# A hybrid decoder step on one core: steps of four chains issued at other ticks, and the last rows scaled by another engine

## The chip, the cores and the metric

The kernel runs on one core of a Trainium2 chip. A core has five engines with a queue of instructions each: TensorE (PE; its weight loads are shown apart as PEld), VectorE (DVE), ScalarE (ACT), GpSimd (POOL) and SyncE (SP), which here does nothing but issue DMAs. An engine takes its instructions in the order of the program and waits, with all that stands behind, when one of them has to wait for another engine or a DMA. The metric is the device time of one execution in microseconds (us), the median of several runs. Nothing is done on the host but to lay out the inputs.

## What is computed

One step of a two-layer decoder in float32 for a prompt of 512 tokens and for 8 samples of one token each (520 columns), width 1024. Cut to what the change comes near:

```python
# layer 0: h = rmsnorm(x) * (1 + scale) + shift;  z = h @ w_in
bg, cg, xv, ga, q, k, v, gb = split(z)
y_a = bg * conv3(cg * xv) * silu(ga)
# prompt: for (window, dilation) in (128,1), (512,4), (2048,16): causal softmax attention,
#         merged by the softmax denominators; samples: one query each against a cached window
y_b = dilated_attention(q, k, v) * silu(gb)
x = x + gate * (concat(y_a, y_b) @ w_out)
# layer 1: same wrapper
u, gc, q, k, v, gd = split(rmsnorm-modulated x @ w_in)
y_c = (pool_mix(u) * pool_scale) * silu(gc)
# retention, 4 heads of 256: prompt in chunks; samples:
new_state = exp(log_g) * state + outer(k, v)
y_d = per_head_norm(q @ state ...) * silu(gd)
x = x + gate * (concat(y_c, y_d) @ w_out)
y = rmsnorm(x, norm_f)
```

Outputs are the two `y`, the appended rows of the convolution, of the windows and of the pooling, and the retention states.

## The kernel before

**Products.** Activations are held transposed: 128 features on the partitions, 520 columns along them. Each weight tile of 1024 x 128 is loaded by SP (`wraw`, 512 KB), split by ACT into a high part (`whi`) and by DVE into a low part (`wlo`), so that float32 accuracy comes from three passes (high x high, high x low, low x high). A product of one weight tile is eight steps k of six matmuls, two column halves times three passes, into one of two PSUM tiles (`mm2`, tag `mm`). So a product needs the PSUM tile of the one before last to have been read. All else on PE uses four smaller PSUM buffers (`aux`).

**Order.** The order of the program is written out by the kernel itself: nothing reorders it. Behind each k step `tick()` counts one tick and issues what is due between the matmuls of the products: everything in `timed` (`at(dt, ...)`), one entry of `side` (`put(..., after=n)`), or, when none of `side` is due, one of `fill` (`put_fill`), and on even ticks one of `aside` (`put2`). So a step's tick is its place in each engine's queue, and all instructions that the step issues, for PE, DVE, ACT or SP, stand at that place.

**Stages, in order of time.**

1. Eight head pairs (`head_pair(p)`), four products each: values, keys, gate, queries. At the end of the query product the pair's attention is put into `side` by ticks counted from there, `Q0 = 5` plus n: two `score` steps (n = 0 and 4), three `turns` (11, 13, 16: PE transposes the softmaxed blocks, ACT makes their high part, DVE their low part a tick or two later), and eight `weigh(e, i)` (L699): values times weights for the pair's two heads e, in four parts i. `weigh(e, 2)` reads group 2, from the last `turns`, `weigh(e, 3)` ends with an ACT copy and a DVE add. They run inside the next pair's products. `q_lo` (L690) is the DVE step that makes the queries' low part and reads the query product's PSUM tile. `ada_two` (32 matmuls for layer 1's modulation) waits in `fill`; for the last pair it is put there 25 ticks after the query product.
2. Layer 0's convolution: 32 products, `a_tile(i, m)` with i from 0, each of which first calls what `hook(i, ...)` left for it. Among them is the softmax of the samples' window scores, in three steps: `soft_scores` (put at i = 5), `soft_turn` and `soft_new`, each put by the one before. `soft_scores` begins with a product of queries and keys on DVE (`prod`), which a matmul with `on_d` sums.
3. Layer 0's output projection (`out_tile`), which sums the squares of the new x (`sqa`).
4. The seam: layer 1's first products run on unnormalised input, while `r1_sums`, `r1_roots` and `rms_rows` make the row factors `r1`, a tick apart, which the evictions (`z_first`) then read. `r1_sums` is put by `at(3, ...)` (L960).
5. Retention, four heads (`ret_head(h)`): values 2 products, keys 2, queries 2, gates 2. The samples' states are loaded four at a time (`state_load`), and `state_new(b0, i)` makes the new state of one sample: ACT scales the old one, DVE makes two products with the v rows `vb`, which have gone through DRAM (`vdr`) to be spread over all partitions; the fourth issues the stores on SP three ticks later. The first four are put into `aside` at the end of the second key product (L1181), the other four after the queries.
6. Pooling, then the output projection of layer 1, whose rows are transposed and scaled by `norm_f` as they come. The last product is done in two column halves; after each, `rows_scale` (L1323) makes 1/rms of its row blocks and scales each block of 128 rows by it, in two half rows (`xo[i][0]`, `xo[i][1]`) that are then stored. The last call is for blocks 0 and 1.

Of the kernel before, what the change touches and what calls it, by code (L numbers as in the profile page):

```python
# [13 lines left out]
ACTF = mybir.ActivationFunctionType  # L14
ALU = mybir.AluOpType
# [3 lines left out]
P = 128  # L19
# [67 lines left out]
def hybrid_kernel(ctx: ExitStack, tc: tile.TileContext, a, o):  # L87
    nc = tc.nc
# [3 lines left out]
    def mk(pool, shape, dt, tag, bufs=None):  # L92
        n_made[0] += 1
        return pool.tile(shape, dt, name=f"{tag}_{n_made[0]}", tag=tag, bufs=bufs)
# [10 lines left out]
    def tt(n=T, dt=F32, p=P):  # L105
        n_made[0] += 1
        return tp.tile([p, 530], dt, name=f"t_{n_made[0]}", tag="t")[:, 0:n]
# [14 lines left out]
    def aux(shape):  # L122
        return mk(auxp, shape, F32, "aux")
# [10 lines left out]
    def act(out, in_, func=ACTF.Copy, bias=None, scale=1.0, accum_out=None):  # L134
        kw = {}
        if bias is not None:
            kw["bias"] = bias
        if accum_out is not None:
            kw["accum_out"] = accum_out
        return nc.scalar.activation(out=out, in_=in_, func=func, scale=scale, **kw)  # L140

    def vcopy(out, in_):
        return nc.vector.tensor_copy(out, in_)  # L143

    def vtt(out, in0, in1, op):
        return nc.vector.tensor_tensor(out=out, in0=in0, in1=in1, op=op)  # L146

    def stt(out, in0, scalar, in1, op0, op1):
        return nc.vector.scalar_tensor_tensor(out=out, in0=in0, scalar=scalar, in1=in1, op0=op0, op1=op1)  # L149

    def vts(out, in0, s1, s2, op0, op1=None):
        if op1 is None:
            return nc.vector.tensor_scalar(out=out, in0=in0, scalar1=s1, scalar2=None, op0=op0)
        return nc.vector.tensor_scalar(out=out, in0=in0, scalar1=s1, scalar2=s2, op0=op0, op1=op1)

    def load(out, in_):
        return nc.sync.dma_start(out=out, in_=in_)

    def mm(out, lhsT, rhs, start, stop):
        nc.tensor.matmul(out, lhsT=lhsT, rhs=rhs, start=start, stop=stop)  # L160
# [23 lines left out]
    def at(dt, fn, *args):  # L184
        seqn[0] += 1
        heapq.heappush(timed, (now[0] + dt, seqn[0], fn, args))

    def put(fn, *args, after=0):
        seqn[0] += 1
        heapq.heappush(side, (now[0] + after, seqn[0], fn, args))  # L190
# [4 lines left out]
    def put2(fn, *args):  # L195
        aside.append((fn, args))
# [316 lines left out]
    def head_pair(p):  # L513
# [182 lines left out]
            put(score, blocks, after=Q0 + n)  # L696
        for g, n in enumerate((11, 13, 16)):
            put(turns, g, after=Q0 + n)
        for e, ticks in ((0, (18, 19, 20, 21)), (1, (22, 23, 24, 26))):  # L699
            for i, n in enumerate(ticks):  # L700
                put(weigh, e, i, after=Q0 + n)

# [7 lines left out]
    for p in range(KT):  # L710
        if p == 6:
            load(scv, a["conv_t"])
        head_pair(p)
# [9 lines left out]

    soft = {}

    def soft_scores():

        prod = tt(P).rearrange("p (b k e) -> p b k e", b=NB, k=KT)
        nc.gpsimd.memset(prod, 0.0)
        for e in range(2):  # L730
            r = slice(64 * e, 64 * e + 64)
            vtt(prod[r, :, :, e].rearrange("p b k -> p k b"), zs[0][r, 32:40, :], zs[0][r, 40:48, :], ALU.mult)
        st = aux([P, 257])
        for t in range(2):
            nc.tensor.transpose(st[:, t * P:(t + 1) * P], scores[:, t].rearrange("p b h -> p (b h)"), ident)
        mm(st[:, 256:257], prod.rearrange("p b k e -> p (b k e)"), on_d[:, 0:1], True, True)
        bd = csm[:, C_BD:C_BD + 257]
        sc = tt(257)
        stt(sc[:, 0:256], st[:, 0:256], 0.125, bd[:, 0:256], ALU.mult, ALU.add)
        stt(sc[:, 256:257], st[:, 256:257], 128.0, bd[:, 256:257], ALU.mult, ALU.add)  # L740
        sm = mk(cp, [P, 2], F32, "sm", 1)
        nc.vector.tensor_reduce(out=sm[:, 0:1], in_=sc, op=ALU.max, axis=AX.X, negate=True)  # L742
        act(sc, sc, ACTF.Exp, bias=sm[:, 0:1], accum_out=sm[:, 1:2])
        nc.vector.reciprocal(sm[:, 1:2], sm[:, 1:2])
        vts(sc, sc, sm[:, 1:2], None, ALU.mult)
        soft["sc"] = sc
        put(soft_turn, after=4)

    def soft_turn():
        sc = soft["sc"]  # L750
        pt_ = aux([P, 2, P])
        for t in range(2):
            nc.tensor.transpose(pt_[:, t, :], sc[:, t * P:(t + 1) * P], ident)
        vcopy(pT[:, :, 0:P], pt_)
        pnr = mk(cp, [P, 64], F32, "pnr", 1)
        vts(pnr, csm[:, C_BCR:C_BCR + 64], sc[:, 256:257], None, ALU.mult)
        soft["pnr"] = pnr
        put(soft_new, after=2)

    def soft_new():  # L760
        pnb = aux([P, 64])
# [53 lines left out]
    def hook(i, fn, *args):  # L815
        hooks.setdefault(i, []).append((fn, args))

    hook(5, put, soft_scores)
    for b0 in range(0, NB, 2):
        i = 5 + 3 * b0 - (2 if b0 else 0)  # L820
# [136 lines left out]
        act(h1[j][0], x)  # L957
        at(2, lo_of, h1[j][1], x, h1[j][0])

    at(3, r1_sums)  # L960
    for j in range(KT):
        at(H1A - 2 + H1B * j, h1_scale, j)
        at(H1A + H1B * j, h1_x, j)
# [21 lines left out]
    def ret_head(h):  # L985
# [192 lines left out]
            for part in range(2):  # L1178
                put(state, i, part, after=5 + (DK if h == 0 else 0))
        for i in range(4):  # L1180
            put2(state_new, 0, i)  # L1181
        for i in range(2):
            if i == 0:
                state_load(4)
# [28 lines left out]
    for h in range(H_D):  # L1213
        ret_head(h)
# [81 lines left out]
    xo = [[tt(512) for _ in range(2)] for _ in range(4)]  # L1296
# [4 lines left out]
    rs = cp.tile([P, 5], F32, name="rs")  # L1301
# [21 lines left out]
    def rows_scale(blocks):  # L1323
        i0, i1 = blocks[0], blocks[-1] + 1
        nc.vector.tensor_reduce(out=rs[:, i0:i1], in_=ss[:, i0:i1], op=ALU.add, axis=AX.X)
        act(rs[:, i0:i1], rs[:, i0:i1], ACTF.Sqrt, bias=eps[:, 0:1])
        nc.vector.reciprocal(rs[:, i0:i1], rs[:, i0:i1])
        for i in blocks:
            if i < 4:
                act(xo[i][0], xo[i][0], ACTF.Copy, scale=rs[:, i:i + 1])  # L1330
                vts(xo[i][1], xo[i][1], rs[:, i:i + 1], None, ALU.mult)
                for hf in range(2):
                    q = nc.scalar if i == 1 else nc.sync
                    q.dma_start(out=o["y_prompt"][0, i * P:(i + 1) * P, hf * 512:(hf + 1) * 512], in_=xo[i][hf])
            else:
                for hf in range(2):
                    vts(xos[hf], xos[hf], rs[0:NB, i:i + 1], None, ALU.mult)
                    load(o["y_sample"].rearrange("b s d -> (b s) d")[:, hf * 512:(hf + 1) * 512], xos[hf])
# [18 lines left out]
    for hf in (1, 0):  # L1357
        ps = mm2()
        for half in (1, 0):
            if hf == 1:  # L1360
                ws.append((take_w(("o", 1, half, m)), yhl[0:KT] if half else yhl[KT:]))
            w, hs = ws[1 - half]
            for k in range(KT):
                mm3(ps, w, k, hs[k][0], hs[k][1], half == 1 and k == 0, half == 0 and k == KT - 1, (hf,))
                if hf == 1:
                    advance(k)
                tick()
        x, g, c = xT[m], mG[1], slice(256 * hf, 256 * hf + 256)
        stt(x[:, c], ps[:, hf, 0:H0], g[:, m, 8:9], x[:, c], ALU.mult, ALU.add)
        if hf == 1:  # L1370
            tmp = mk(cp, [P, NB], F32, "gtmp", 2)
            vtt(tmp, ps[:, 1, H0:H0 + NB], g[:, m, 0:NB], ALU.mult)
            vtt(x[:, S:T], tmp, x[:, S:T], ALU.add)
        blocks = range(2) if hf == 0 else range(2, 5)
        at(4, rows, m, blocks)
        at(6, rows_scale, blocks)
# [71 lines left out]
```

## Time and profile before

| | |
|---|---|
| median of 3 runs (lowest, highest) | 1060.53 us (1060.45, 1061.29) |
| the profiled execution's own time | 1060.99 us |
| its span, from the first to the last instruction | 1058.9 us |
| mean granted clock of TensorE | 0.997 |
| read from HBM, written to it | 149.40 MB, 18.65 MB |

By the first matmul of each product the stages lie in the span about so: head pairs 26 to 285 (the last pair's attention runs on to 319), convolution 285 to 499, output projection 499 to 596, retention 596 to 849, pooling 849 to 953, the last projection 953 to 1050, scaling and storing to the end.

A row of a timeline is the start, the length, the engine, line, operation, the tiles written and read, their size, how many instructions were merged, and in brackets the idle time of the engine before it and what ended it. A row of the waits is the engine and line that waited, what it waited for, the total, how often, and the longest. A row of the windows gives for a stretch the busy time and number of instructions of PE, PEld, DVE, ACT and POOL, then the granted clock, the share of the DMA engines and GB/s. Lines are those of helpers (L160 every matmul, L140 every activation, L146 two-input DVE operations, L149 fused ones, L153 scalings), so the tiles tell the places apart.

### The profile page before, as it was taken

How to read it: one execution, taken by the hardware profiler on the slowest of the kernel's cores; microseconds unless marked ns; L12 is line 12 of the kernel's file. 1: busy time of each engine (PE TensorE's matmuls, PEld its weight loads, DVE VectorE, ACT ScalarE, POOL GpSimd, SP SyncE). 2: the span in 40 equal slices, each digit the busy share in tenths (PEclk: the TensorE clock that was granted, in tenths of full speed). 3: DMA queues.
4: the chain of work that ended last, by engine and by line, in shares of the span. 5: the costliest groups of instructions: out<-in, count | busy, mean ns of one | idle time of the engine just before them, and what ended most of it. 6: DMA issues, size and time to landing. Idle time of an engine off the chain costs nothing.

```text
span 1058.9 us, 21054 instructions
## 1 busy us (share of the span) xinstructions
PE 1034.0 (98%) x8682; PEld 989.6 (93%) x8682; DVE 623.8 (59%) x1470; ACT 485.6 (46%) x884; POOL 4.3 (0%) x33
## 2 busy tenths in 40 slices
PE   5999999999999999999999999999999999999996
PEld 3899999999999999999999998999999999999996
DVE  5656777667775444456344586665657576674443
ACT  5666567765654222224232474445444453333333
POOL 0000000000000000000000000000000000000000
PEclk9999999999999999999999999999999999999998
DMA  9576664576626635613744255363726523225322
GB/s 352 213 248 200 180 171 158 172 212 189 192 88 197 191 109 185 199 61 141 238 147 138 100 168 197 109 203 113 263 81 212 164 78 129 81 80 172 101 71 81
DMA packets 82175, 168.95 MB, mean 160 GB/s; under 512 B 7208, under 2 KB 47240, under 8 KB 79000
## 3 DMA queue, kind: packets, MB, share of 16 engines
q1 hardware_dynamic: 81792, 167.09, 49.0%
q8 instruction: 68, 1.11, 0.4%
q10 hardware_dynamic: 288, 0.52, 0.1%
q14 instruction: 27, 0.22, 0.1%
HBM read 149.40 MB, written 18.65 MB: 159 GB/s over the span
## 4 chain that ended last, share of the span: by engine, by line
PE 64%; DVE 2%; ACT 1%; DMA 1%; issue 0%; DVEq 0%; ACTq 0%
PE mm L160 55%; PE aux L160 8%; DVE t L146 1%; DMA v<-vdr 1%; DVE wlo L146 0%; ACT t L140 0%; PE aux L1318 0%; DVE big L149 0%; DVE t L149 0%; ACT whi L140 0%; PE aux L999 0%; PE aux L992 0%; DMA vdr<-t 0%; ACT v L140 0%; PE aux L374 0%
## 5 line engine op out<-in xcount | busy, mean ns | idle before, releaser
L160 PE MATMUL mm<-t,whi 128*128 128x256 f32 (+1 forms) x4608 | 755.0, 285 | 1.1 <-DVE zs L143 0.9
L160 PEld LDWEIGHTS mm<-t,whi 128*128 128x128 f32 x4608 | 636.2, 188 | 17.6 <-issue 13.6
L160 PE MATMUL mm<-t,wlo 128*128 128x256 f32 (+2 forms) x2304 | 465.4, 282 | 0.0
L160 PEld LDWEIGHTS mm<-t,wlo 128*128 128x128 f32 x2304 | 358.1, 188 | 0.0
L146 DVE TENSOR_TENSOR wlo<-wraw,whi 128x512 fp32r<-128x512 f32 x288 | 189.0, 683 | 57.7 <-ACT whi L140 57.0
L140 ACT ACTIVATE whi<-wraw 128x1024 fp32r<-128x1024 f32 x144 | 151.7, 1053 | 96.4 <-PE mm L160 53.9
L146 DVE TENSOR_TENSOR t<-t,t 128x520 fp32r<-128x520 f32 (+6 forms) x182 | 119.0, 657 | 98.7 <-ACT t L140 97.0
L140 ACT ACTIVATE t<-t 128x520 fp32r<-128x520 f32 (+3 forms) x116 | 71.0, 616 | 161.3 <-DVE t L149 102.9
L140 ACT ACTIVATE t<-aux 128x384 fp32r<-128x384 f32 (+7 forms) x156 | 67.8, 465 | 135.3 <-PE aux L160 79.1
L140 ACT ACTIVATE t<-mm 128x512 f32<-128x512 f32 (+2 forms) x116 | 56.2, 506 | 116.2 <-PE mm L160 114.8
L146 DVE TENSOR_TENSOR t<-aux,t 128x384 fp32r<-128x384 f32 (+6 forms) x120 | 58.4, 494 | 33.2 <-ACT t L140 28.3
L160 PE MATMUL aux<-t,v 128*128 128x512 f32 (+2 forms) x224 | 51.2, 327 | 1.1 <-DVE t L146 0.6
L160 PE MATMUL aux<-t,t 64*128 64x256 f32 (+6 forms) x384 | 51.9, 320 | 0.0
L143 DVE COPY zs<-mm 128x8 f32<-128x8 f32 x76 | 12.0, 158 | 64.5 <-ACT t L140 64.5
L160 PEld LDWEIGHTS aux<-t,t 64*128 64x128 f32 (+1 forms) x384 | 41.5, 186 | 3.9 <-issue 1.7
L140 ACT ACT_TABLE_LOAD x32 | 41.1, 1283 | 4.5 <-DVE sm L742 2.2
L160 PEld LDWEIGHTS aux<-t,v 128*128 128x128 f32 x224 | 35.1, 188 | 3.8 <-DVE t L146 2.7
L140 ACT ACTIVATE t<-t,mn 128x128 f32<-128x128 f32 (+3 forms) x64 | 35.1, 551 | 0.1
L149 DVE SCALAR_TENSOR_TENSOR big<-v,ksc,big 128x256 f32<-128x256 f32 x64 | 27.7, 480 | 12.0 <-ACT big L140 9.8
L146 DVE TENSOR_TENSOR t<-mm,t 128x512 f32<-128x512 f32 (+1 forms) x24 | 16.5, 689 | 30.4 <-PE mm L160 22.8
L591 DVE CUSTOM_DVE_ANT_0 t<-aux,t 128x128 f32<-128x128 f32 (+3 forms) x64 | 27.5, 486 | 10.7 <-PE aux L160 10.7
L146 DVE TENSOR_TENSOR gtmp<-mm,mG 128x8 f32<-128x8 f32 x16 | 2.6, 165 | 44.4 <-PE mm L160 44.4
(153 smaller groups left out, 552.4 us busy)
## 6 DMA issues: line engine op xcount, KB each, us to landing
wraw<-in_w_in_e SPq DMA_DIRECT2D x64, 512.0 KB, 3.9
wraw<-in_w_in_o SPq DMA_DIRECT2D x48, 512.0 KB, 3.4
big<-in_ada_e SPq DMA_DIRECT2D x12, 1024.0 KB, 8.6
big<-in_ada_o SPq DMA_DIRECT2D x12, 1024.0 KB, 10.3
wraw<-in_w_out_e SPq DMA_DIRECT2D x16, 512.0 KB, 3.3
big<-in_state_ret SPq DMA_DIRECT2D x16, 512.0 KB, 7.2
out_new_ret_sample<-big SPq DMA_DIRECT2D x16, 512.0 KB, 3.0
wraw<-in_w_out_o SPq DMA_DIRECT2D x16, 512.0 KB, 4.3
```

What stands on the lines that cost most here:

```text
L140: return nc.scalar.activation(out=out, in_=in_, func=func, scale=scale, **kw)
L143: return nc.vector.tensor_copy(out, in_)
L146: return nc.vector.tensor_tensor(out=out, in0=in0, in1=in1, op=op)
L149: return nc.vector.scalar_tensor_tensor(out=out, in0=in0, scalar=scalar, in1=in1, op0=op0, op1=op1)
L160: nc.tensor.matmul(out, lhsT=lhsT, rhs=rhs, start=start, stop=stop)
L591: nc.vector.tensor_tensor_reduce(out=sb, in0=s[:, 0:n], in1=bt[e][:, S - n:S], scale=1.0, scalar=3e38, op0=ALU.add, op1=ALU.min, accum_out=mn,
```

## The change

Four things are moved in the program's order, and the last scaling is divided otherwise.

- `weigh`: the parts of the first head are issued 18, 19, 21 and 22 ticks after `Q0` in place of 18, 19, 20 and 21, those of the second 23, 24, 25 and 27 in place of 22, 23, 24 and 26.
- The softmax: `prod` becomes a step of its own, `soft_prod`, which the fifth convolution product (i = 4) calls; `soft_turn` comes eight ticks after `soft_scores` (four before) and `soft_new` four after that (two before).
- `r1_sums` comes at the fourth tick in place of the third.
- `state_new` for the first four samples: with h = 0 it is put into `aside` eight ticks later, for other heads one tick later.
- `rows_scale`: ACT scales only the first half row of the odd blocks (1 and 3) and issues its store; DVE scales all other half rows, and SP issues their stores. Before, ACT scaled the first half row of each block and DVE the second, and SP issued all stores but those of block 1, which ACT issued.

```diff
-        for e, ticks in ((0, (18, 19, 20, 21)), (1, (22, 23, 24, 26))):
+        for e, ticks in ((0, (18, 19, 21, 22)), (1, (23, 24, 25, 27))):
             for i, n in enumerate(ticks):
                 put(weigh, e, i, after=Q0 + n)
...
-    def soft_scores():
+    def soft_prod():
 
         prod = tt(P).rearrange("p (b k e) -> p b k e", b=NB, k=KT)
         nc.gpsimd.memset(prod, 0.0)
         for e in range(2):
             r = slice(64 * e, 64 * e + 64)
             vtt(prod[r, :, :, e].rearrange("p b k -> p k b"), zs[0][r, 32:40, :], zs[0][r, 40:48, :], ALU.mult)
+        soft["prod"] = prod
+
+    def soft_scores():
+
+        prod = soft["prod"]
         st = aux([P, 257])
...
-        put(soft_turn, after=4)
+        put(soft_turn, after=8)
...
-        put(soft_new, after=2)
+        put(soft_new, after=4)
...
+    hook(4, soft_prod)
     hook(5, put, soft_scores)
...
-    at(3, r1_sums)
+    at(4, r1_sums)
...
         for i in range(4):
-            put2(state_new, 0, i)
+            at(1 if h else 8, put2, state_new, 0, i)
...
             if i < 4:
-                act(xo[i][0], xo[i][0], ACTF.Copy, scale=rs[:, i:i + 1])
-                vts(xo[i][1], xo[i][1], rs[:, i:i + 1], None, ALU.mult)
                 for hf in range(2):
-                    q = nc.scalar if i == 1 else nc.sync
-                    q.dma_start(out=o["y_prompt"][0, i * P:(i + 1) * P, hf * 512:(hf + 1) * 512], in_=xo[i][hf])
+                    dst = o["y_prompt"][0, i * P:(i + 1) * P, hf * 512:(hf + 1) * 512]
+                    if i % 2 and hf == 0:
+                        act(xo[i][hf], xo[i][hf], ACTF.Copy, scale=rs[:, i:i + 1])
+                        nc.scalar.dma_start(out=dst, in_=xo[i][hf])
+                    else:
+                        vts(xo[i][hf], xo[i][hf], rs[:, i:i + 1], None, ALU.mult)
+                        load(dst, xo[i][hf])
```

## The prediction

> **What bounds the kernel.** First the page: the share of each engine and the granted clock. Then who kept TensorE (PE) waiting, all over the span.
>
> ```profile
> span 1058.9 us, 21054 instructions
> PE 1034.0 (98%) x8682; PEld 989.6 (93%) x8682; DVE 623.8 (59%) x1470; ACT 485.6 (46%) x884; POOL 4.3 (0%) x33
> PEclk9999999999999999999999999999999999999998
> ```
>
> ```profile
> PE aux L160 <- DMA t<-in_x_t: 8.3, 1, 8.3
> PE aux L160 <- DVE t L146: 1.6, 4, 0.6
> PE mm L160 <- DVE zs L143: 0.9, 2, 0.7
> PE aux L753 <- DVE t L153: 0.6, 1, 0.6
> PE aux L1318 <- DVE t L149: 0.6, 1, 0.6
> PE aux L160 <- DVE pnr L153: 0.3, 1, 0.3
> ```
>
> PE is busy for 98% of the span at full granted clock, so no edit of DVE or ACT work counts by its own length: it counts where PE waits for it, or behind PE's last matmul. The columns of the waits are the total, how often, and the longest. The first row lies in the kernel's start, which the change doesn't touch. What is left is some 4 us in nine short waits, and the change touches most of the places. So the question is what those waits really cost, and whether moving the steps makes new ones.
>
> **How long a short wait is.** Here are three rows of PE's timeline in the last head pair (start, length, operation, and the idle time before it).
>
> ```profile
> 308.67 0.28 PE L160 MATMUL aux<-t,v 128*128 128x256 f32 x1
> 309.53 0.39 PE L160 MATMUL aux<-t,v 128*128 128x256 f32 x1 [0.59 <-DVE t L146]
> 310.48 0.40 PE L160 MATMUL aux<-t,v 128*128 128x256 f32 x2
> ```
>
> Two of these matmuls take 0.40, one takes 0.28, so undisturbed ones start 0.12 apart and each overlaps the next by 0.16. Across the wait the starts lie 0.86 apart, 0.74 more than 0.12, while the row prints 0.59. A wait therefore costs its printed idle time plus 0.16, and one under 0.16 prints nothing. I price every wait below so. The Trainium skill, Perfetto Trace Analysis, section "Identifying the Most-Contended Engine", says that matmul busy time misleads because matmuls are pipelined, and takes the weight loads' busy share instead; the 0.59 against 0.74 here agrees, and by its measure the next term would be 2.7 in place of 2.35 and the whole sum 6.9.
>
> **Weighted values, L699 (eight head pairs).** In each pair `weigh(0, 2)` needs the low part of the third group's transposes, which DVE makes late.
>
> ```profile
> PEld aux L160 <- DVE t L146: 2.7, 8, 0.8
> 314.75 1.93 PE L160 MATMUL aux<-big,scT 128*32 128x256 f32 x32
> big<-in_ada_o SPq DMA_DIRECT2D x12, 1024.0 KB, 10.3
> ```
>
> The first row is of the waits of PE's weight loads between 52 and 318 us: eight, one for each pair, 2.7 in all. The longest, 0.8, is the one above, 0.74 by its starts; I take 0.05 off each, so the other seven are 1.9 - 0.35 = 1.55, and with the last 0.75 I get 2.3. One tick is one k step of a product, six matmuls, 0.72. `weigh(0, 2)` issued a tick later finds the low part done in seven pairs (their mean wait is 0.22) and just about in the last. No instruction is added. What slides is the end: `weigh(1, 3)` now comes in the last tick of the query product, so its ACT copy stands before the query's eviction on ACT, and its DVE add before `q_lo`; I cost this at nothing, and its price is the fourth rival. In the last pair `ada_two` waits in `fill` for a free tick: before, that was tick 30 (the x32 row at 314.75), now it is 25, the tick freed in front of `weigh(0, 2)`. Its 1.93 of PE work and one ACT copy only change places; its weights are asked for 28 ticks, 20 us, ahead, and such a load takes 10.3 by the page's row above, so they are there. It gives `weigh(0, 2)` 1.9 more slack.
>
> **The convolution's softmax, L726 to L758.** PE stalls three times in one chain; the last row is DVE's.
>
> ```profile
> 326.17 0.35 PE L160 MATMUL aux<-on_d,t 128*128 128x1 f32 x2 [0.47 <-DVE t L146]
> 330.12 0.44 PE L753 MATMUL aux<-csm,t 128*128 128x128 f32 x2 [0.61 <-DVE t L153]
> 332.30 0.44 PE L160 MATMUL aux<-pnr,csm 128*128 128x64 f32 x2 [0.31 <-DVE pnr L153]
> 325.50 0.52 DVE L146 TENSOR_TENSOR t<-zs 64x64 f32<-64x64 f32 x2
> ```
>
> 0.47 + 0.61 + 0.31 and three times 0.16 make 1.87. `soft_prod` takes the two products (0.52) out of the chain and issues them eight ticks, 5.8, before the matmul that reads them; its fill on POOL goes past one or two short fills of that queue, which works 4.3 in the whole span by the page, so it delays none of them. `soft_turn` comes four ticks later, 2.9 against a wait of 0.77, and `soft_new` two more, 1.4 against 0.47. The next reader, the windows' weighing, is due at tick 65 and the chain now ends at 53. The 0.52 stays on DVE, beside PE's products. None of the three issues a DMA. I take all of 1.87 as gone.
>
> **Row sums of the seam, L960.**
>
> ```profile
> 599.08 1.28 PE L160 MATMUL aux<-on_d,t 128*128 128x1 f32 x10 [0.32 <-DVE t L146]
> 603.59 0.70 DVE L146 TENSOR_TENSOR t<-t,t 128x520 f32<-128x520 f32 x1 [0.34 <-ACT t L140]
> 605.40 0.69 DVE L149 SCALAR_TENSOR_TENSOR t<-mm,t 128x512 f32<-128x512 f32 x1 [1.11 <-PE mm L160]
> ```
>
> The wait is 0.48; one tick of 0.72 covers it. What is late next is `r1`, by 0.72 - 0.48 = 0.24: its first reader at 603.59 moves by that, and the first eviction that reads it (605.40) waits for PE by 1.11 anyway. Gain 0.48.
>
> **The first head's state, L1181.** PE rows, then DVE rows, the last one a group of the page (busy, mean ns of one).
>
> ```profile
> 638.74 0.72 PE L160 MATMUL mm<-t,whi 128*128 128x256 f32 x4 [0.74 <-DVE zs L143]
> 639.91 0.51 PE L160 MATMUL aux<-v,t 128*128 128x256 f32 x2 [0.21 <-ACT t L140]
> 640.63 0.74 PE L160 MATMUL aux<-v,t 128*128 128x256 f32 x4 [0.22 <-DVE t L146]
> 643.35 1.56 PE L160 MATMUL aux<-t,t 128*128 128x512 f32 x6
> 633.45 0.88 DVE L149 SCALAR_TENSOR_TENSOR big<-v,ksc,big 128x256 f32<-128x256 f32 x2 [1.32 <-DMA v<-vdr]
> 637.84 0.68 DVE L146 TENSOR_TENSOR t<-mm,t 128x512 fp32r<-128x512 f32 x1
> 638.44 0.15 DVE L143 COPY zs<-mm 128x8 f32<-128x8 f32 x1
> 641.70 0.68 DVE L146 TENSOR_TENSOR t<-mm,t 128x512 fp32r<-128x512 f32 x1
> L146 DVE TENSOR_TENSOR wlo<-wraw,whi 128x512 fp32r<-128x512 f32 x288 | 189.0, 683 | 57.7 <-ACT whi L140 57.0
> ```
>
> DVE stands 1.32 for the v rows that come back through DRAM, then makes four pairs of products before the first query's low part (637.84) and its sample copy (638.44); PE waits for that copy to get its PSUM tile back, then twice for k's split behind it: 0.74 + 0.21 + 0.22 and 0.48 make 1.65. Between 633.45 and 637.84 lie 4.39: the four pairs, some 0.8 each, and two weight splits (683 ns alone, some 0.6 in a row). With h = 0 put off by eight ticks, one pair stands before that copy and three behind it, and the splits fill the 1.32 of waiting: the copy ends at 638.59 - 2.4 - 1.2 = 635.0, ahead of PE's need near 637.9. What is late next: the second query's low part (641.70, done at 642.4), now behind the other three pairs; the work ahead of it is the same but 1.2 of idling is gone, so it ends near 641.2, and the first score, then at 643.35 - 1.65 = 641.7, needs it some 0.7 into its 1.56. Slack about 1. The two stores on SP follow their last step, six ticks later, past one weight load, which is asked for four tiles ahead. Other heads: steps leave the list on even ticks only, so one tick's delay leaves them where they were. Gain 1.65.
>
> **The tail, L1328.** ACT and DVE scale rows, SP and ACT issue the last four stores; below them the windows' row of the DMAs (the last number is GB/s).
>
> ```profile
> 1052.97 1.33 ACT L140 ACTIVATE t<-t,rs 128x512 f32<-128x512 f32 x2 [0.23 <-DVE rs L1327]
> 1052.97 0.88 DVE L153 TENSOR_SCALAR t<-t,rs 128x512 f32<-128x512 f32 x2
> 1053.72 0.83 SPq L1334 DMA_DIRECT2D out_y_prompt<-t  x2
> 1054.34 0.87 ACTq L1334 DMA_DIRECT2D out_y_prompt<-t  x2
> 1055.00:1056.00 1.00, 0.00 (x0) 0.00 (x0) 0.00 (x0) 0.00 (x0) 0.00 (x0) 0.50 1.03 383
> ```
>
> A half row takes ACT about 0.72 and DVE 0.48 (0.40 to the next). Before, the first store waits for ACT, 1053.72; now for DVE, 1053.48: 0.24 earlier. The last issue goes from 1054.80 (ACT's second) to 1054.40 (SP's third): 0.40 earlier. The DMA engines are full while the four stores run, 1 MB at 383 GB/s is 2.7, longer than the issues; so the start counts, 0.24, and 0.40 is the other end. DVE's extra half row among the earlier blocks (five in place of four, 0.40) ends near 1050.1, before the residual at 1050.34 that waits for PE. The Trainium skill, DMA: Bandwidth & Descriptors, section "Issuing engines are not separate DMA queues", says that DMAs of several issuers share the same engines and that a second issuer saves only issue time; this speaks against giving SP three of four. The trace agrees: with 383 GB/s moving, the issues (0.83 for two) run ahead of the data.
>
> **The sum.** 2.3 + 1.87 + 0.48 + 1.65 + 0.24 = 6.5. The profiled execution took 1060.99 (span 1058.9 and 2.1 around it), which would become 1054.5; the median of the runs is 0.46 lower, 1060.53, so 1054.0 is what a median should show.
>
> **The rivals.**
> 1. The state's steps still stand in front of something (0.10). One step now sits directly before the first query's low part; if the v rows land 2 us later than at 633.4, or the other three pairs hold the second query's low part past the score, up to 1.65 stays: 1055.7. For it: a slack of about 1 only. Against: the same DVE work with less idling.
> 2. `ada_two` takes over the wait of the last pair (0.12). In its new tick it needs a PSUM buffer; if that is one whose last reader is the late low part, PE waits there as it did for `weigh(0, 2)`, 0.75: 1054.8. Against: of four buffers only two have that reader.
> 3. The waits only move (0.10): the change doesn't do what it says, as DVE is behind by its own load, and PE, once ahead, waits at the next low part. DVE is busy 185.18 of the 266.00 us of the pairs' stage, by the windows' row:
>
> ```profile
> 52.00:318.00 266.00, 264.88 (x2237) 250.26 (x2236) 185.18 (x470) 167.34 (x336) 0.56 (x5) 1.00 0.60 181
> ```
>
> If the pairs' 2.3 and the state's 1.65 stay: 1057.9; if half of the rest too, 1059.2, within what counts as no change. Against: 30% of idle DVE time there, and waits of 0.2 that a tick outlasts.
> 4. Slower, by one mechanism (0.05): `weigh(1, 3)` in the last tick delays `q_lo`. ACT's copy (0.59) and DVE's add (a pass of 0.69) now stand before it, and the next pair's scores, five ticks (3.6) after the query product, wait for it; seven pairs times 1.28 are 9.0, less 6.5 gained, 1063.0. It decides when `q_lo` ends later than the scores' last third, which reads it. In one pair the copy, `q_lo` and the scores stand so:
>
> ```profile
> 153.88 0.59 ACT L140 ACTIVATE t<-aux 64x512 f32<-64x512 f32 x1 [4.29 <-PE aux L160]
> 155.94 0.69 DVE L149 SCALAR_TENSOR_TENSOR t<-mm,t 128x512 fp32r<-128x512 f32 x1
> 158.17 0.98 PE L160 MATMUL aux<-t,t 64*128 64x256 f32 x12
> ```
>
> `q_lo` ends 1.5 before even the scores' start, more than the 1.28: that speaks against it.
>
> **How the numbers follow.** The forecast, all five terms, has 0.63; the rivals have 0.10, 0.12, 0.10 and 0.05. The range takes in the forecast and the first two rivals, with both at once (1056.4) and 0.4 for the runs' spread; below, the sum by weight loads (6.9), the tail's other end (0.16) and 0.5 of spread: 1053.0 to 1056.9. A difference under 0.2%, 2.1 us, can't be told from none here. Faster by more: forecast, first two rivals and a part of the third, 0.89; same 0.06; slower 0.05.
>
> **What would show it.** Right: no wait of weight loads on DVE between 52 and 318; no idle before the on_d, transposing and pnr matmuls near 326 to 332; none at the row sums; no zs wait near 638; the first of the last four stores 0.24 earlier after the last matmul. Wrong: a wait before the x32 matmuls in the last pair, before the 64-row scores, or before the 128x512 scores of the first head.

## The result and the profile after

| | before | after |
|---|---|---|
| median of the runs (lowest, highest, n) | 1060.89 us (1060.45, 1061.29, 4) | 1053.29 us (1053.20, 1054.51, 4) |
| the profiled execution | 1060.99 us | 1053.25 us |
| its span | 1058.9 us | 1051.1 us |

The ratio is 0.9928, with an interval of 0.9916 to 0.9940: the change takes off 7.6 us, against the 6.5 of the forecast. The page of the changed kernel answers the first rows of the prediction:

```profile
span 1051.1 us, 21056 instructions
PE 1030.5 (98%) x8682; PEld 989.8 (94%) x8682; DVE 623.4 (59%) x1472; ACT 484.1 (46%) x882; POOL 4.3 (0%) x33
PEclk9999999999999999999999999999999999999999
```

The work is the same: as many matmuls, the clock full, DVE's and ACT's busy times changed by 1.5 us at most. The span became shorter by 7.8. Now the waits of PE, all over the span (total, how often, longest):

```profile
PE aux L160 <- DMA t<-in_x_t: 8.4, 1, 8.4
PE aux L348 <- ACT md L140: 3.2, 2, 1.7
PE aux L1324 <- DVE t L149: 0.6, 1, 0.6
PE aux L160 <- DMA big<-in_ada_e: 0.5, 2, 0.3
PE aux L160 <- DVE rc L412: 0.3, 1, 0.3
PE mm L160 <- DVE t L146: 0.2, 1, 0.2
PE mm L160 <- DVE zs L143: 0.2, 1, 0.2
```

Behind the first 52 us only two of these rows are left: L1324, in the tail, which was there before (as L1318), and `rc` on L412, which is new. All others lie in the kernel's start. The weight loads have no wait on DVE any more between 52 and 318 us.

**Where the 7.8 came from.** Both programs issue the same products in the same order, 48 matmuls each, so the start of each product can be compared in both traces. The places below go by the starts of the 144 products (the fifth is the first of the second head pair, the 81st the first of retention). The table gives the time from one start to the next named one.

| stretch | before | after | gained | forecast |
|---|---|---|---|---|
| to the 5th product | 57.56 | 57.52 | 0.04 | 0 |
| 5th to 37th (pairs, to the last one's attention) | 261.18 | 258.12 | 3.06 | 2.3 |
| 37th to 41st (the softmax chain) | 26.14 | 23.95 | 2.19 | 1.87 |
| 41st to 81st (convolution, output projection) | 251.51 | 251.64 | -0.13 | 0 |
| 81st to 82nd (seam) | 8.80 | 8.67 | 0.13 | 0.48 |
| 82nd to 89th (first head, its state) | 57.75 | 55.76 | 1.98 | 1.65 |
| 89th to 144th (retention, pooling, projection) | 381.20 | 380.99 | 0.21 | 0 |
| 144th to the end (tail) | 14.72 | 14.43 | 0.29 | 0.24 |

Three terms came out larger than forecast, by some 0.1 for each wait, and the seam fell nearly out. (The last pair's attention ends a little behind the 37th product: 0.10 of the 2.19 is still its share, as the first experiment shows.) Those are the two things to explain. In what follows "offset" is the start of a product against the changed kernel's, counted from the fifth product, so that the kernel's start is left out.

### The profile page after: what moved, and what is told of

It is laid out like the page before. It is cut to its first block, busy times and chain, and to the rows that moved or that the text cites. A ratio compares the mean times of both kernels' runs of the same rounds, so it can differ in the third digit from the quotient of the medians.

```text
span 1051.1 us, 21056 instructions
## 1 busy us (share of the span) xinstructions
PE 1030.5 (98%) x8682; PEld 989.8 (94%) x8682; DVE 623.4 (59%) x1472; ACT 484.1 (46%) x882; POOL 4.3 (0%) x33
## 4 chain that ended last, share of the span: by engine, by line
PE 94%; DVE 2%; ACT 1%; issue 0%; DVEq 0%; ACTq 0%
PE mm L160 78%; PE aux L160 13%; PE aux L615 2%; ACT t L140 1%; DVE t L146 1%; PE aux L1324 0%; DVE wlo L146 0%; PE aux L998 0%; PE aux L519 0%; PE aux L1005 0%; PE aux L374 0%; ACT md L140 0%; ACT whi L140 0%; DVE mS L153 0%; DVE mA L154 0%
## 5 line engine op out<-in xcount | busy, mean ns | idle before, releaser
L160 PE MATMUL aux<-t,v 128*128 128x512 f32 (+2 forms) x224 | 49.0, 323 | 0.0
```

## What the experiments showed

Each is an edit of the changed kernel. The medians also hold the differences between the starts of executions (second experiment below), so what is less than 1 us is read from offsets, each from one profiled execution.

| run | median us (lowest, highest) | ratio to before, interval | offset at the end, us |
|---|---|---|---|
| e1_pairs_back | 1057.25 (1055.95, 1058.60) | 0.9960 (0.9945, 0.9975) | +3.11 |
| e2_soft_back | 1058.09 (1056.43, 1058.20) | 0.9964 (0.9950, 0.9978) | +2.67 |
| e3_state_back | 1057.19 (1056.13, 1057.63) | 0.9958 (0.9943, 0.9973) | +1.62 |
| e4_rows_later | 1053.88 (1052.70, 1054.87) | 0.9928 (0.9913, 0.9943) | -0.54 |
| e0_after | 1054.15 (1053.23, 1056.11) | 0.9927 (0.9913, 0.9941) | -0.01 |
| e5_sums_back | 1054.54 (1053.14, 1056.62) | 0.9927 (0.9905, 0.9949) | +0.12 |
| e6_tail_back | 1053.82 (1053.62, 1056.28) | 0.9927 (0.9909, 0.9945) | +0.22 |
| e7_no_slide | 1054.39 (1053.08, 1056.40) | 0.9929 (0.9910, 0.9948) | -0.11 |
| e8_ada_back | 1054.19 (1053.54, 1055.73) | 0.9923 (0.9909, 0.9938) | +0.44 |
| e9_tail_two | 1053.76 (1053.41, 1054.12) | 0.9917 (0.9902, 0.9932) | -0.02 |
| e10_both | 1052.70 (1052.45, 1052.95) | 0.9908 (0.9892, 0.9925) | -0.65 |
| e11_slots | 1056.07 (1055.31, 1056.83) | 0.9939 (0.9919, 0.9959) | +1.52 |

**The pairs' waits alone.** The ticks of `weigh` are put back.

```diff
-        for e, ticks in ((0, (18, 19, 21, 22)), (1, (23, 24, 25, 27))):
+        for e, ticks in ((0, (18, 19, 20, 21)), (1, (22, 23, 24, 26))):
```

> The changed kernel with the ticks of weigh as before; all else as changed. Theory A: a wait of PE costs its lateness and a fixed restart: the waiting matmul then runs with its weight load in the open, 0.39 long where others are 0.28, so printed idle + 0.16 + 0.11. Eight waits come back: 2.39 by their starts and 8 x 0.11, together 3.1 to 3.3 us slower than the changed kernel, about 1056.4, with matmuls of 0.39 behind the waits in the eight pairs. Rival B, the price of the prediction (printed idle + 0.16, no restart): 2.3 slower, 1055.6. Rival C, the waits only move: under 1 slower.

The offset is +0.39 at the ninth product, +3.05 at the 37th and +3.16 at the 41st, when the last pair's attention is through. The same steps stand between the kernels before and after. The eight waits of the weight loads between 52 and 320 us are back:

```profile
PEld aux L160 <- DVE t L146: 2.8, 8, 0.8
```

The timeline of this kernel's last pair shows one of them (PEld rows are weight loads, each of the matmuls in the PE row behind it):

```profile
310.08 0.28 PE L160 MATMUL aux<-t,v 128*128 128x256 f32 x1
...
310.95 0.19 PEld L160 LDWEIGHTS aux<-t,v 128*128 128x128 f32 x1 [0.80 <-DVE t L146]
310.95 0.38 PE L160 MATMUL aux<-t,v 128*128 128x256 f32 x1 [0.60 <-DVE t L146]
311.06 0.55 PEld L160 LDWEIGHTS mm<-t,whi 128*128 128x128 f32 x4
311.18 0.65 PE L160 MATMUL mm<-t,whi 128*128 128x256 f32 x4
```

Look at the starts. The load of `whi` begins 0.12 before its matmul, while the matmul ahead of it still runs. At the wait, load and matmul begin together, at 310.95: that load was not done ahead. The matmul then takes 0.38 in place of 0.28, and the next one starts 0.23 behind it in place of 0.12. So a wait is followed by a restart of 0.11, which the idle time in front of it can't show. The Trainium skill, TensorE: Matmul & The Clock Gate, section "Step-by-step: what each phase is for", says that PE pulls weight loads ahead of running matmuls, when the row groups don't conflict or the load goes to a background weight buffer, while the matmuls stay in order; the 0.12 of lead agrees, and it is lost at the wait. The 2.3 of the prediction and eight restarts make 3.2, against 3.16 here. The trace gives both parts apart: over its eight waits the waiting matmuls start 2.38 later than 0.12 behind the one ahead, and those behind them 0.83, 0.10 each, 3.21 together. Theory A, the restart, holds; the prediction's own price does not. Only the longest of the eight prints an idle time in PE's rows: the first one's matmul is 0.30 late, and nothing is printed.

**The changed kernel again.**

> The changed kernel again, beside the others. The four kernels of the first call began their products 1 to 2 us later in the span than the changed kernel's profile, before any edited place, at waits for the first loads. Theory F: that start varies from execution to execution of one program, so this one lies anywhere between 1053.2 and 1055.5 us and its products' starts, counted from the fourth product on, agree with the first profile of it within 0.3. Rival: the later start belongs to the edits; then this one starts as the first profile did and is at 1053.3.

The profiled execution took 1056.11. The fifth product starts 2.91 later than in the first profile, and from there on every product start agrees within 0.02. The first row of PE's waits shows a part of it:

```profile
PE aux L160 <- DMA t<-in_x_t: 9.8, 1, 9.8
```

It was 8.4 in the first profile, 1.4 less. The other 1.5 comes in the matmuls behind that load, which take longer in this execution until some 22 us. Here are the same 16 of them in the first profile and in this one:

```profile
14.19 1.07 PE L160 MATMUL aux<-big,scT 128*32 128x256 f32 x16
16.23 1.93 PE L160 MATMUL aux<-big,scT 128*32 128x256 f32 x16
```

The trace's record of a full granted clock begins at 13.4 us in the first profile and at 22.2 in this one, just where the rows come back to their length, so the clock is the likely reason; no run tries it. Theory F holds: executions differ in their first 30 us, and the rest of one program repeats. So an offset of 0.1 is real; whether it is the edit's own is another question, which the last but one experiment takes up.

**The softmax chain alone.**

```diff
+        soft_prod()
         prod = soft["prod"]
...
-        put(soft_turn, after=8)
+        put(soft_turn, after=4)
...
-        put(soft_new, after=4)
+        put(soft_new, after=2)
...
-    hook(4, soft_prod)
```

> The changed kernel with soft_prod called inside soft_scores again, soft_turn after four ticks and soft_new after two. Theory A: three waits and three restarts, 1.87 + 0.33 = 2.2 slower than the changed kernel, 1055.5. Rival B: 1.9 slower, 1055.2. Rival C: under 0.7 slower. The waits are expected at the on_d, the transposing and the pnr matmuls, as in the kernel before.

+2.31 at the 41st product. PE's timeline has all three waits again:

```profile
325.43 0.35 PE L160 MATMUL aux<-on_d,t 128*128 128x1 f32 x2 [0.69 <-DVE t L146]
329.38 0.44 PE L759 MATMUL aux<-csm,t 128*128 128x128 f32 x2 [0.61 <-DVE t L153]
331.57 0.43 PE L160 MATMUL aux<-pnr,csm 128*128 128x64 f32 x2 [0.30 <-DVE pnr L153]
```

The same three places in the timeline of the changed kernel have none:

```profile
322.33 0.28 PE L160 MATMUL aux<-on_d,t 128*128 128x1 f32 x2
328.32 0.38 PE L758 MATMUL aux<-csm,t 128*128 128x128 f32 x2
331.44 0.33 PE L160 MATMUL aux<-pnr,csm 128*128 128x64 f32 x2
```

The printed idle is 1.60, with 0.16 each 2.08, with 0.11 each for the restart 2.41. 2.31 lies nearer to the price with restart. The lengths say how large a restart is with these shapes: 0.35, 0.44 and 0.43 behind a wait, 0.28, 0.38 and 0.33 without, so 0.07, 0.06 and 0.10. With these 0.23 the 2.08 becomes 2.31. The offset grows to 2.66 by the 81st product, in the output projection, which this edit doesn't touch.

**The state alone.**

```diff
-            at(1 if h else 8, put2, state_new, 0, i)
+            put2(state_new, 0, i)
```

> The changed kernel with the first head's state steps put into the list at once, as before. Theory A: the zs wait and two behind it with restarts, 1.65 + 0.3 = 1.95 slower than the changed kernel, 1055.2. Rival B: 1.65 slower, 1054.9. Rival C: under 0.6 slower.

+1.63, at first sight the prediction's 1.65. But the waits are not those of before:

```profile
634.93 0.72 PE L160 MATMUL mm<-t,whi 128*128 128x256 f32 x4 [0.45 <-DVE zs L143]
636.10 0.51 PE L160 MATMUL aux<-v,t 128*128 128x256 f32 x2 [0.21 <-ACT t L140]
636.82 0.73 PE L160 MATMUL aux<-v,t 128*128 128x256 f32 x4 [0.22 <-DVE t L146]
```

The first printed 0.74 in the kernel before. 0.88 of idle and three times 0.16 make 1.36; three restarts more, 1.69. Only the second fits 1.63. The number alone would have spoken for the wrong price. It is less than the 1.98 of the table because the first wait came back shorter.

**The seam: what took the place of the wait.** Rows of the timeline in the kernel before:

```profile
600.92 0.69 DVE L146 TENSOR_TENSOR wlo<-wraw,whi 128x512 fp32r<-128x512 f32 x1 [0.27 <-ACT whi L140]
601.53 0.18 DVE L412 RECIPROCAL rc<-rc 128x5 f32<-128x5 f32 x1
601.79 1.26 PE L160 MATMUL aux<-csm,rc 128*128 128x128 f32 x10
```

And in the changed kernel:

```profile
594.16 1.17 PE L160 MATMUL aux<-on_d,t 128*128 128x1 f32 x10
595.64 0.25 ACT L140 ACTIVATE rc<-aux,eps 128x5 f32<-128x5 f32 x1
595.76 1.29 DVE L146 TENSOR_TENSOR wlo<-wraw,whi 128x512 fp32r<-128x512 f32 x2 [0.27 <-ACT whi L140]
596.98 0.18 DVE L412 RECIPROCAL rc<-rc 128x5 f32<-128x5 f32 x1
597.21 1.28 PE L160 MATMUL aux<-csm,rc 128*128 128x128 f32 x10 [0.30 <-DVE rc L412]
```

The row sums (`on_d`) no longer wait. But `rms_roots` is due one tick behind them and now stands on DVE behind both halves of a weight split, 1.29, in place of one, 0.69. The reciprocal comes 2.82 after the start of the sums, before it was 2.45, and `rms_rows`' matmuls wait for it: 0.30 printed, in place of 0.32. Two runs try both sides. The first puts the sums back, the second gives the roots one tick more:

```diff
-    at(4, r1_sums)
+    at(3, r1_sums)
```

> The changed kernel with r1_sums at the third tick again. Theory D (the tick only swapped one wait of PE for another): the row sums wait as before (0.3 printed), the reciprocal's wait goes, and the products behind the seam start 0.0 to 0.2 later than in the changed kernel, counted from its start. Rival (the prediction's term): 0.48 to 0.6 later.

```diff
-        at(1, rms_rows, rms_roots(pc), r1)
+        at(2, rms_rows, rms_roots(pc), r1)
```

> The changed kernel with rms_rows two ticks after r1_roots instead of one. In the trace of the changed kernel rms_rows waits 0.30 for the reciprocal (L412), which stands behind both halves of a weight split on DVE. Theory D (the seam's gain was eaten by this new wait): the wait goes, 0.30 + 0.16 + 0.11 = 0.57 faster than the changed kernel, 1052.7, and r1's first eviction still waits for PE. Rival E (r1 is then late and the first evictions hold the PSUM tiles): no gain or slower, with a zs or PSUM wait in the seam's second or third product.

Sums put back: +0.12 at the 82nd product, with the row sums' wait in place of the reciprocal's. So the edit brought 0.12, not 0.48. Roots later: -0.58 at the 82nd product, and no new wait behind it, against rival E. In that kernel's trace the split and the reciprocal stand as before, and PE comes by later:

```profile
597.82 1.29 DVE L146 TENSOR_TENSOR wlo<-wraw,whi 128x512 fp32r<-128x512 f32 x2 [0.27 <-ACT whi L140]
599.03 0.18 DVE L412 RECIPROCAL rc<-rc 128x5 f32<-128x5 f32 x1
599.53 1.18 PE L160 MATMUL aux<-csm,rc 128*128 128x128 f32 x10
```

0.30 + 0.16 + 0.11 = 0.57, measured 0.58: theory D holds on both sides. Why 0.12 was left is in the rows' lengths. In the kernel before the `rc` matmuls print no wait, yet their row takes 1.26, against 1.18 here, where nothing is late: 0.08 of lateness and restart stood there already, too short to print. The row sums took 1.28 with their wait and take 1.17 without, a restart of 0.11. So the seam lost 0.32 + 0.16 + 0.11 + 0.08 = 0.67 before and 0.30 + 0.16 + 0.10 = 0.56 after, 0.11 less.

**The slide, `ada_two` and the tail.** These asked whether what the prediction put at nothing was nothing. First, `weigh(1, 3)` a tick before the last, as if nothing had slid:

```diff
-        for e, ticks in ((0, (18, 19, 21, 22)), (1, (23, 24, 25, 27))):
+        for e, ticks in ((0, (18, 19, 21, 22)), (1, (23, 24, 25, 26))):
```

> The changed kernel with weigh(1, 3) at 26 after Q0 in place of 27, so that it doesn't come in the last tick of the query product. The prediction cost that slide at nothing: the products start as in the changed kernel within 0.1 over the eight pairs, counted from the start. Rival 4 of the prediction (the slide delays q_lo and the scores): some 0.1 to 1 faster for each pair.

The offset is -0.12 after seven pairs and -0.14 at the 41st product, without a printed wait between 52 us and the seam in either kernel. So the slide costs 0.14 at most, against the 9.0 of the fourth rival. It can't be told from nothing: in the output projection, which it doesn't touch, the same offset moves by another -0.23. Second, the last `ada_two` behind `weigh(0, 2)` again:

```diff
-                at(20 if p < KT - 1 else 28, put_fill, ada_two, ...
+                at(20 if p < KT - 1 else 33, put_fill, ada_two, ...
```

> The changed kernel with the last pair's ada_two put into fill five ticks later, so that it comes behind weigh(0, 2) as before and not in front of it. The prediction held that weigh(0, 2), one tick later, finds its low part just about done even so: 0 to 0.3 later from the last pair on, counted from the start. Rival 2 of the prediction (ada_two in front costs): up to 0.75 earlier. Rival H (it was ada_two in front that took the last pair's wait away, and a tick alone doesn't): 0.5 to 0.8 later, with a wait at weigh(0, 2) in the last pair.

+0.17 after the last pair, within the 0 to 0.3 of the expectation, and no wait at `weigh(0, 2)`: a tick alone was enough. In the changed kernel the 32 matmuls run, and behind them `weigh`, with no wait before either:

```profile
306.45 1.93 PE L160 MATMUL aux<-big,scT 128*32 128x256 f32 x32
...
309.12 0.40 PE L160 MATMUL aux<-t,v 128*128 128x256 f32 x2
```

Third, the tail as it was, and fourth, two stores on each queue with the new scaling:

```diff
-                    if i % 2 and hf == 0:
-                        act(xo[i][hf], xo[i][hf], ACTF.Copy, scale=rs[:, i:i + 1])
-                        nc.scalar.dma_start(out=dst, in_=xo[i][hf])
...
+                act(xo[i][0], xo[i][0], ACTF.Copy, scale=rs[:, i:i + 1])
+                vts(xo[i][1], xo[i][1], rs[:, i:i + 1], None, ALU.mult)
+                    q = nc.scalar if i == 1 else nc.sync
```

> The changed kernel with the scaling and the stores of the last rows as before. Theory G (the stores are held by the DMA engines' rate from the first one on): the end comes 0.24 to 0.3 later after the last matmul of the products than in the changed kernel. Rival (by the last issue): 0.40 later.

```diff
-                        load(dst, xo[i][hf])
+                        (nc.scalar if i == 1 else nc.sync).dma_start(out=dst, in_=xo[i][hf])
```

> The changed kernel with both stores of block 1 issued by ACT, two and two, with the scaling as changed. Theory G (the DMA engines are full from the first store on): the end comes within 0.05 of the changed kernel's after the last product. Rival (the last issue sets the end): some 0.2 earlier, as SP's third issue goes.

The old tail costs 0.23 from the last product on; the second issuer brings 0.01. The changed kernel's last rows, scalings and issues, and the windows' row of the DMAs behind them:

```profile
1045.53 0.72 ACT L140 ACTIVATE t<-t,rs 128x512 f32<-128x512 f32 x1 [0.23 <-DVE rs L1333]
1045.53 1.28 DVE L153 TENSOR_SCALAR t<-t,rs 128x512 f32<-128x512 f32 x3
1046.04 1.46 SPq L157 DMA_DIRECT2D out_y_prompt<-t  x3
1046.28 0.34 ACTq L1340 DMA_DIRECT2D out_y_prompt<-t  x1
1048.00:1049.00 1.00, 0.00 (x0) 0.00 (x0) 0.00 (x0) 0.00 (x0) 0.00 (x0) 0.50 1.04 393
```

The first store goes out 0.51 after the scalings begin, before it was 0.75 (1053.72 less 1052.97): 0.24. SP's three issues take 1.46; with two on each queue the last issue ends 0.32 earlier, for 0.01. So the issues don't set the end, as theory G has it; the DMA engines are full behind them, with 393 GB/s. The rule of the Trainium skill that the prediction weighed here (DMA: Bandwidth & Descriptors, section "Issuing engines are not separate DMA queues") agrees with that 0.01.

**The rest that no wait explains.** The table of the stretches has -0.13 and +0.21 where the change touches nothing. One run takes one more buffer ahead of the head pairs, filled by POOL and read by nobody, so that each later tile of that pool gets another buffer:

```diff
     ada_w = {}
+    nc.gpsimd.memset(tt(), 0.0)
```

> The changed kernel with one more buffer taken, filled by POOL and given back before the head pairs, which shifts by one which buffer each later tile gets; no other work is added. Profiles of one program agree within 0.02 from the fourth product on, but those of edited programs drift by 0.1 to 0.4 in stages without any wait, in the distance between matmuls. Theory K (the drift comes with the buffers' places): drifts of 0.1 to 0.5 in stages that have no wait. Rival: none over 0.05.

The offset is at most 0.18 up to the 89th product, then +0.43 at the 97th, +0.81 at the 113th and +1.45 at the 129th: 0.74 in retention and 0.64 in pooling, more than the 0.1 to 0.5 expected. PE's waits behind the start are the changed kernel's own (L1325 is its L1324). Below them are the windows' rows of the pooling stage, in the changed kernel and here:

```profile
PE aux L1325 <- DVE t L149: 0.6, 1, 0.6
PE aux L160 <- DVE rc L412: 0.3, 1, 0.3
842.10:945.00 102.90, 102.90 (x859) 102.42 (x858) 71.64 (x162) 40.55 (x65) 0.73 (x7) 1.00 0.27 88
844.90:948.40 103.50, 103.50 (x858) 103.02 (x857) 71.67 (x161) 40.53 (x65) 0.73 (x7) 1.00 0.27 87
```

PE is busy all the time at a granted clock of 1.00 in both, its weight loads pause for 0.48 in both, and the stage is 0.6 longer. So matmuls follow each other a little more slowly with no wait that the trace shows, as theory K has it. In pooling, over 256 pairs of starts, a matmul of 256 columns from `whi` is followed by its 264-column partner after 118.4 ns on average in the changed kernel, after 120.9 here, and after 120.8 in the kernel before. Not every pair goes that way: from that partner to the next 256-column matmul from `whi` it is 123.0 in the changed kernel and 121.5 here, over 128 pairs. Where buffers lie thus moved the time by 1.5 us in this run, the only one of its kind. Other edits show drifts like it in the output projection, which they don't touch: -0.23 in e1, +0.35 in e2, -0.23 in e7. That this is also the -0.13 and the +0.21 is likely, since `soft_prod` takes its buffer earlier, but it was not tried; and by what means a place acts wasn't tried either. An offset of some 0.3 is thus the edit's own only where it arises at the edited place itself.

**A faster version.** The roots a tick later, and the last residual in two parts of 128 columns, so that the rows' first transposes wait for half of it:

```diff
-        at(1, rms_rows, rms_roots(pc), r1)
+        at(2, rms_rows, rms_roots(pc), r1)
...
-        stt(x[:, c], ps[:, hf, 0:H0], g[:, m, 8:9], x[:, c], ALU.mult, ALU.add)
+        for b in range(2):
+            cb = slice(256 * hf + P * b, 256 * hf + P * b + P)
+            stt(x[:, cb], ps[:, hf, P * b:P * b + P], g[:, m, 8:9], x[:, cb], ALU.mult, ALU.add)
```

> The changed kernel with rms_rows two ticks after r1_roots, and the last residual made in two parts of 128 columns so that the first transpose can start before the second part is done. The first is worth 0.60 by its own run. The second: the wait in front of the last transposes is 0.58 printed; a part takes some 0.35, so the first block's transposing comes 0.1 to 0.2 earlier, and ACT, which takes 0.4 for each block, is not held by the second. Together 0.6 to 0.8 faster than the changed kernel, counted from the start of the products; by the median 1052.5 to 1053.6, as the start varies.

1052.70 against 1053.76 of e9_tail_two, which by offsets is the changed kernel, on the same chip; its ratio to the kernel before is 0.9908 (0.9892 to 0.9925). By offsets 0.65 of that is the edit's; the rest fits the start (in the profiled executions the fifth product comes at 57.40 against 57.90). Of the 0.65, 0.52 is there at the last product, and 0.13 comes behind it, where the wait is now

```profile
PE aux L1324 <- DVE t L149: 0.4, 1, 0.4
```

in place of 0.6.

## Why the prediction was right, and where not

- **What bounds the kernel: right.** PE at full clock, and a few short waits on DVE. e1, e2 and e3 each bring back waits at their own places and nowhere else, and the time for them.
- **The price of a wait: too low.** "A wait therefore costs its printed idle time plus 0.16" left out the restart, 0.11 each. It was in sight: of the three rows quoted, the waiting matmul takes 0.39 and the undisturbed one 0.28. Eight waits in the pairs, three in the softmax and three in the state make 14 x 0.11 = 1.5. The terms with it are 3.2, 2.20 and 1.98; measured were 3.16, 2.09 and 1.98, with the 0.10 behind the 37th product counted to the pairs. The softmax's restarts were shorter, as e2 shows. The measure by weight loads, 6.9 for the sum, is too low as well.
- **The seam: the step that failed** is "What is late next is `r1`, by 0.72 - 0.48 = 0.24". It followed the readers of `r1`, and not what stands ahead of the reciprocal on DVE. With a tick more, `rms_roots` fell behind the second half of a weight split too, and a wait of 0.30 came up one step earlier in the chain. 0.12 of 0.48 was gained.
- **The state: right in its mechanism.** The copy `zs` was to end at 635.0 and the second query's low part near 641.2. This stage now stands 5.3 earlier, so at 629.7 and 635.9. Below are DVE's rows in the changed kernel's timeline, and then PE's first score:

```profile
626.74 1.28 DVE L146 TENSOR_TENSOR wlo<-wraw,whi 128x512 fp32r<-128x512 f32 x2
627.95 0.87 DVE L149 SCALAR_TENSOR_TENSOR big<-v,ksc,big 128x256 f32<-128x256 f32 x2
628.74 0.68 DVE L146 TENSOR_TENSOR t<-mm,t 128x512 fp32r<-128x512 f32 x1
629.34 0.15 DVE L143 COPY zs<-mm 128x8 f32<-128x8 f32 x1
...
634.98 0.68 DVE L146 TENSOR_TENSOR t<-mm,t 128x512 fp32r<-128x512 f32 x1
```

```profile
636.08 1.55 PE L160 MATMUL aux<-t,t 128*128 128x512 f32 x6
```

  They end at 629.49 and 635.66, with two weight splits and one pair of products ahead of the copy, as worked out. The low part is done 0.42 before the score begins, and by the prediction's 0.7 into the score 1.1 ahead of need, the "slack about 1" of the forecast: the first rival did not come.
- **What was put at nothing** was nearly so: the slide at most 0.14 (e7), `ada_two` 0.17 on the good side (e8).
- **The tail: right**, 0.24 forecast and 0.23 by e6. The table's 0.29 has 0.06 more, which e6, with the tail as before, doesn't give back.
- **The rivals.** The second and third would have left a wait in the pairs, the fourth several us there; neither PE nor its weight loads wait for DVE or ACT between 52 us and the seam.

The sum by these corrections: 6.5 and 1.5 for the restarts, less 0.36 at the seam, is 7.6, against 7.7 by the starts from the fifth product on. The undersized price and the seam pulled in opposite directions, and the larger error was on the careful side: 1.1 to 1.2 too little gain forecast. How far the median lies from 1054.0 says less: it was 1053.29 at first and 1054.15 when the same kernel ran again, since the start moves, so where it falls in the stated range is in part luck.

## What to carry to other kernels

Price a short wait of TensorE from starts, and through the matmul behind it: here idle, 0.16 of lost overlap and 0.11 of restart, 0.27 on top of what the row prints, and 0.22 to 0.26 with the softmax's shapes; a matmul 0.30 late printed nothing. When a step is issued later, go down each queue that its successors use and see what they now stand behind: the seam's chain lost three quarters of its gain to a weight split on DVE. Where executions differ by more than the effect, compare the starts of the same products and leave the kernel's start out; and read an edit's effect at its own place, since stages it doesn't touch can drift by some tenths.

## What the runs showed of the hardware

- After a wait the weight load isn't ahead of its matmul any more, and the next matmul comes 0.11 later with 128x128 weights and 256 columns (310.95 to 311.18 in place of 0.12); over e1's eight waits it is 0.83.
- Two executions of one program agree within 0.02 us in the starts of their products over 990 us, from the fifth on; the first 30 us shifted the whole by 2.9 us, 1.4 by the first load and 1.5 by matmuls that took longer until some 22 us (1.93 in place of 1.07).
- The place of buffers changes the spacing of matmuls without a wait that the trace shows: 118.4 against 120.9 ns for one kind of pair, 123.0 against 121.5 for another, 1.5 us over the kernel in e11.
